# Nine extra contiguous products leave the TensorE stream, and eleven of its large products get another column order

## The chip, the cores and the metric

The kernel runs on one core of one Trainium2 chip. The metric is the device time of one execution in microseconds (us). Each time given for a kernel is the median of several executions; one more execution is taken with the hardware profiler and has a time of its own.

## The reference

One decoder layer (depth 1, model width 2048) is applied to 256 prompt rows and to 8 x 8 = 64 sample rows that share all weights, so 320 rows in all:

```python
xn = rms_norm(x, g_mix)
b_gate, c_gate, h_conv, q, k, v, gate_c, gate_a = split(xn @ w_in)
y_conv = (b_gate * dwconv3(c_gate * h_conv)) @ w_conv_out
y_attn = window_attention(q, k, v, rel_bias, sinks) @ w_attn_out      # window 128, 16 heads, 4 kv heads
h = x + (sigmoid(gate_c) * y_conv + sigmoid(gate_a) * y_attn) @ w_o
hn = rms_norm(h, g_ffn)
h = h + (silu(hn @ w_gate) * (hn @ w_up)) @ w_down                    # inner width 5632
y = rms_norm(h, g_final)
```

The prompt attends in two blocks of 128 queries; the sample rows attend to a cached window of 128 keys and their own 8. Beside y the kernel returns the updated key, value and convolution windows. All data is float32.

## The kernel before, in words

Every large product has the weights as the stationary operand (128 x 128) and all 320 rows as the moving one: 320 columns a matmul. To keep float32 accuracy both sides are split into a rounded part and a remainder, and three products are summed in PSUM: `whi` by `xh_t`, `whi` by `xl_t`, `wlo` by `xh_t`. The weights stream from HBM in 512 KB pieces on SP's queue into `wraw`; ScalarE (ACT) makes `whi`, VectorE (DVE) makes `wlo` (`split_to`, L128 to L130).

TensorE's (PE's) program runs in the order in which it is written. `kv_product` forms keys and values (tiles of 1, 1, 1, 1, 2, 2, ... chunks of 128 features; `k0` is the first chunk of a tile), then come the four products for `q`, then `C`, `H`, `B` in turn four times, then eight rounds of `gc`, `ga`, `yc`, `ya` (gates and the two output projections), `wo`, and two halves of the feed-forward network (`fg`, `fu`, then `dn` for the down projection). All but `kv` and `dn` go through `product` (its matmul is L186; that of `kv` is L372).

Attention is side work: a generator that `tick` advances by one step behind each loaded weight tile. `prompt_attention` has eight units (two heads of one kv head each): `prompt_scores` puts six matmuls of 256 columns (`ps`) into the stream, `prompt_pv` twice 24 small ones (`po`), `sample_attention` 64 scores (`pss`) and 72 value products (`spo`).

Two details matter here. First, the 320 rows lie as five segments of 64, 64 columns of one chunk following those of the last, so that one chunk's moving operand is five runs of 64 elements with a fixed step (`fives`, `rows_in`). Second, `turns` sets the order in which a large product visits its columns: four from the first segment, four from the second, ... and, after all five, the next four of each. PSUM is written in the same order. Matmuls in the program's rows read 128x16x5x4 in that order and 128x320 where the columns are written straight through.

`nudge` (L205 to L207) is a matmul that computes nothing which is used: a contiguous run of 320 elements of `xh_t` by a contiguous 128 of `xl_t` (or `hh_t`, `hl_t`), into a tile of the four-deep `aux` PSUM pool that nobody reads. It stands in nine places: at `k0` of 6 in `kv_product`, before the third `q` product, twice behind `prompt_pv`, behind the last unit's scores, behind the sample's scores, behind the sample's values, and ahead of the first `fu` product of either half.

Of the kernel before, what the change touches and what calls it, by code (L numbers as in the profile page):

```python
# [17 lines left out]
T = TP + NB * TS  # L18
# [8 lines left out]
P = 128  # L27
# [25 lines left out]
def hybrid_layer(ctx: ExitStack, tc: tile.TileContext, a: dict, o: list):  # L53
    nc = tc.nc
# [17 lines left out]
    def ps_aux(name):  # L72
        return aux[0].tile([P, 512], F32, tag="aux", name=name)
# [3 lines left out]
    def u(s):  # L77
        uid[0] += 1
        return f"{s}_{uid[0]}"
# [21 lines left out]
    def turns(ap):  # L101

        return ap.rearrange("p s (i b) -> p i s b", b=4)

    def fives(ap):

        return ap.rearrange("p (s j) -> p s j", s=NS)
# [24 lines left out]
    def load_cols(w, k0, n, c0, behind=()):  # L132
# [4 lines left out]
            split_to(hi[:, :n, :], lo[:, :n, :], raw[:, :n, :])  # L137
        return hi, lo

    mark = {}  # L140
    side_work = [None]
    pending = []
    last = {}
# [28 lines left out]
    def product(load, nk, xh, xl, name, tiles=None, loaded=None):  # L172

        ps = [ps_acc(u(name)) for _ in range(2)]
        k0 = 0
        for n in tiles or [min(KT, nk - k) for k in range(0, nk, KT)]:
            hi, lo = load(k0, n)
            if loaded:
                loaded()
            order = [(k, c) for k in range(n) for c in range(2)]  # L180
            if k0 + n == nk:
                order.sort(key=lambda kc: kc[1])
            for k, c, i in passes(order, k0 + n == nk):
                kc = k0 + k
                w, x = ((hi, xh), (hi, xl), (lo, xh))[i]
                last["mm"] = nc.tensor.matmul(  # L186
                    turns(fives(ps[c][:, :T])), w[:, k, c * P:(c + 1) * P], turns(x(kc)),
                    start=(kc == 0 and i == 0), stop=(kc == nk - 1 and i == 2),
                )
            k0 += n  # L190
            while pending:
                with after(last["lo"], last["mm"]):
                    pending.pop(0)()
            tick()
        return ps

    def two_parts(src, tags=("ta", "tb")):
# [3 lines left out]
        nc.scalar.activation(hi, src, AF.Copy)  # L201
        nc.vector.tensor_sub(lo, src, hi.bitcast(F32))
        return hi, lo

    def nudge(rows, weights, n=T):  # L205
        x, w = (bass.AP(r.tensor, r.offset, [list(r.ap[0]), [1, m]]) for r, m in ((rows(0), n), (weights(0), P)))
        nc.tensor.matmul(ps_aux(u("nudge"))[:, :n], w, x, start=True, stop=True)  # L207

    def over_partitions(out, parts):
        for i, x in enumerate(parts):  # L210
# [48 lines left out]
    xh, xl = row_tiles(xp, ("xh_t", "xl_t"), KC, LEAD_X, ("xh", "xl"))  # L259
# [26 lines left out]
    def x_load(i, eng=nc.sync):  # L286
# [11 lines left out]
        out=ident, in_=ident, compare_op=ALU.not_equal, fill=1.0, base=0, pattern=[[-1, P]],  # L298
# [47 lines left out]
    def kv_product(tiles, x_after):  # L346

        ps = [ps_acc(u("kv")) for _ in range(4)]
        k0 = 0
        x_prep(0)  # L350
        for i, n in enumerate(tiles):
            if k0 == 6:
                nudge(xh, xl)
            hi, lo = load_kv(k0, n)
            if i == 0:
                x_prep(1)
            for b in x_after.get(i, ()):
                x_load(b)
            order = [(k, c) for k in range(n) for c in range(4)]
            if k0 + n == KC:  # L360
                order.sort(key=lambda kc: kc[1])
            seq = passes(order, k0 + n == KC)
            if i == 0:
                seq.sort(key=lambda kcm: kcm[2])
            for k, c, m in seq:
                kc = k0 + k
                if k0 and (k, c, m) == (0, 3 if n > 1 else 1, 0) and k0 + n < KC:
                    for kk in range(tiles[i + 1]):
                        x_prep(k0 + n + kk)
                    tick()  # L370
                w, x = ((hi, xh), (hi, xl), (lo, xh))[m]
                last["mm"] = nc.tensor.matmul(  # L372
                    turns(fives(ps[c][:, :T])), w[:, k, c * P:(c + 1) * P], turns(x(kc)),
                    start=(kc == 0 and m == 0), stop=(kc == KC - 1 and m == 2),
                )
            k0 += n
            if i == 0:
                tick()
        return ps
# [88 lines left out]
    def at_rows(part):  # L468
# [15 lines left out]
        out=sides[:, 0], in_=sides[:, 0], compare_op=ALU.is_ge, fill=0.0, base=-1, pattern=[[-1, WIN]],  # L484
# [158 lines left out]
    def prompt_attention():  # L643
        units = [(j * 2 + par, gp) for j in range(2) for gp in range(2) for par in range(2)]
        bias, sc, sm, turned, pts = {}, {}, {}, {}, {}
        bias[0] = bias_load(*units[0])
        for i in range(len(units) + 3):
            if i < len(units):
                if i + 1 < len(units):
                    bias[i + 1] = bias_load(*units[i + 1])  # L650
                sc[i] = prompt_scores(*units[i], bias.pop(i))
                if i + 1 == len(units):
                    nudge(xh, xl)
                yield
                sm[i] = prompt_softmax(*units[i], sc[i])
            if 0 <= i - 3 < len(units):
                pts[i - 3] = prompt_sides(i - 3, turned.pop(i - 3))
            yield
            if i >= 4 and i % 4 == 2:
                for n in (i - 5, i - 3):  # L660
                    kv, gp = units[n]
                    prompt_pv(kv // 2, gp, (pts.pop(n - 1), pts.pop(n)))
                nudge(xh, xl)
            if 0 <= i - 1 < len(units):
                turned[i - 1] = prompt_norm(i - 1, sc.pop(i - 1), *sm.pop(i - 1))
            yield
# [3 lines left out]
    def sample_attention(sm):  # L670
# [3 lines left out]
        s = sm.tile([P, NB, W2], F32, name="s_s")  # L674
# [6 lines left out]
        for base in range(0, NB, 3):  # L681
            ps = ps_aux(u("pss"))
            n = min(3, NB - base)
            for b in range(base, base + n):
                o0 = (b - base) * W2
                for kv in range(NKV):
                    j, par = kv // 2, kv % 2
                    rows = slice(par * 64, par * 64 + 64)
                    nc.tensor.matmul(
                        ps[kv * 32:(kv + 1) * 32, o0:o0 + W2], qs[rows, j, b, :], kf[rows, b, j, :],  # L690
                        start=True, stop=True,
# [2 lines left out]
                s[:, base:base + n, :], ps[:, 0:n * W2].rearrange("p (b k) -> p b k", b=n),  # L694
                flip(bias_s).unsqueeze(1).to_broadcast([P, n, W2]),
            )
        nudge(xh, xl)
        yield
        yield

# [49 lines left out]
        for j in range(2):  # L750
            for par in range(2):
# [4 lines left out]
                    start=True, stop=False,  # L756
                )
        for b in range(NB):
            cv = cvs.pop(b)
            for j in range(2):  # L760
                for par in range(2):
# [3 lines left out]
                        cv[:, kv * HD:(kv + 1) * HD], ptw[:, kv, b * 32:(b + 1) * 32],  # L765
                        start=False, stop=(b == NB - 1),
                    )
        nudge(xh, xl)
        yield
        for j in range(2):  # L770
            src = pos[j][:, 0:256].rearrange("p (b g t) -> p g b t", b=NB, g=GRP)
            o = LEAD_A + j * 4 * at_row
            rows = at_t[:, o:o + 4 * at_row].rearrange("p (g w) -> p g w", g=GRP)[:, :, -2 * JS:]
# [42 lines left out]
    for j in range(2):  # L816
        for gp in range(2):
            if (j, gp) == (1, 0):
                nudge(xh, xl)
            ps = in_pair(O_Q + (j * 2 + gp) * CW, "q")  # L820
            pending.append(lambda j=j, gp=gp, ps=ps: q_out(j, gp, ps))
    side_work[0] = attention()
# [2 lines left out]
    for cp in range(4):  # L825
        c_sb = []
        ps = in_pair(O_C + cp * CW, "C")
# [4 lines left out]
        ps = in_pair(O_H + cp * CW, "H")  # L832
        conv = []
        for c in range(2):
# [13 lines left out]
            n = UL - 2  # L848
# [10 lines left out]
        ps = in_pair(O_B + cp * CW, "B")  # L859
# [17 lines left out]
    mm = mp_.enter_context(tc.tile_pool(name="mm", bufs=1, side="right"))  # L877
# [9 lines left out]
    for mp in range(8):  # L887
        c0 = mp * CW
        sg = {}
        for nm, off, tag in (("gc", O_GC, "ta"), ("ga", O_GA, "tb")):  # L890
            ps = in_pair(off + c0, nm)
# [26 lines left out]
    for mp in range(8):  # L918
# [5 lines left out]
        for c in range(2):  # L924
            k = mp * 2 + c
# [101 lines left out]
    for half in range(2):  # L1027
# [4 lines left out]
        for fpair in range(nf // 2):  # L1032
            c0 = (f0 + fpair * 2) * P
            psg = product(
                lambda k0, n: load_cols(w_g, k0, n, c0), KC,
                hh, hl, "fg",
            )
            if half == 0 and fpair == 0:
                pss = ps_aux("pss2")
                over_partitions(pss[:, :T], two_parts(hacc, ("tc", "td")))  # L1040
                rstd_of(pss[:, :T], [P, T], "r2", hp, out=rb2)
            gs = []
            for c in range(2):
                t, t2 = tmp("ta", "gs")[:, :T], tmp("tb", "sg")[:, :T]
                nc.vector.tensor_mul(t, psg[c][:, :T], rb2)
                last["sig"] = nc.scalar.activation(t2, t, AF.Sigmoid)
                nc.vector.tensor_mul(t, t, t2)
                nc.vector.tensor_mul(t, t, rb2)
                gs.append(t)
            if fpair == 0:  # L1050
                nudge(hh, hl)
            psu = product(
                lambda k0, n: load_cols(w_u, k0, n, c0), KC,
                hh, hl, "fu",
            )
            for c in range(2):
                nc.vector.tensor_mul(gs[c], psu[c][:, :T], gs[c])
                f = fpair * 2 + c
                (first, rest), row = parts_of(gs[c]), a_move(f)
                nc.scalar.activation(row[:, :, JR:JT], rest, AF.Copy)  # L1060
                last["hi"] = nc.scalar.activation(row[:, :, 0:JR], first, AF.Copy)
                nc.vector.tensor_sub(row[:, :, JT:], rest, row[:, :, JR:JT].bitcast(F32))
                last["lo"] = nc.vector.tensor_sub(placed(a_low(f)), first, row[:, :, 0:JR].bitcast(F32))
                if half == 1:
                    nc.scalar.activation(a_first(f), gs[c][:, 0:P], AF.Copy)
# [109 lines left out]
    for c in range(4):  # L1175
        k = E0 // P + c
# [147 lines left out]
```

## Time and profile before

| | before |
|---|---|
| median of 3 runs | 1593.76 us (1593.33 to 1593.9) |
| the profiled execution's own time | 1593.85 us |
| its span, first to last instruction | 1592.1 us |
| PE busy | 1583.2 us, 99% of the span |
| PE's weight loads busy | 1547.1 us |
| DVE, ACT busy | 890.9 us, 645.9 us |
| granted TensorE clock | 0.998 |

Matmuls overlap: a product of 320 columns shows 301 ns from its start to its end, and the next starts 140 ns after it. So busy time is a union of overlapping pieces, and the pace of the stream is read from starts: from the chain of waits, which merges consecutive work of one line into a row of start, length and count (the rows' starts are ends of the work before them, so they lie some 0.16 us behind the starts of the timeline), and from the timeline.

### The profile page before, as it was taken

The page shows a single profiled execution, that of the slowest core. Times are in us where ns is not written, and L with a number is a line of the kernel's source. Part 1 is how long each engine was busy: PE and PEld are TensorE (multiplying, and loading weights), DVE is VectorE, ACT ScalarE, POOL GpSimd, SP SyncE. Part 2 cuts the span into 40 slices and gives each one's busy share as a digit, 9 for nine tenths or more (in the row PEclk, how much of TensorE's full clock was granted, in tenths as well). Part 3 has the DMA queues.
Part 4 walks back from the last instruction along what each step waited for, and adds up shares of the span by engine and source line. Part 5 has one row for each costly group of instructions (what it writes and reads, how often), then busy time and mean ns, then how long its engine had stood idle before and what let it go on. Part 6 is the DMA issues. An engine that isn't in the chain of part 4 may idle for free.

```text
span 1592.1 us, 26453 instructions
## 1 busy us (share of the span) xinstructions
PE 1583.2 (99%) x10899; PEld 1547.1 (97%) x10899; DVE 890.9 (56%) x1314; ACT 645.9 (41%) x917; POOL 133.2 (8%) x213
## 2 busy tenths in 40 slices
PE   9999999999999999999999999999999999999998
PEld 9999999999999999999999999998888999999887
DVE  7879765445555445556555555553444455555556
ACT  7554443333333333344333333333333334444443
POOL 1414332000000003320000000000000000000021
PEclk9999999999999999999999999999999999999999
DMA  7757566544455544455554545555555454445663
GB/s 271 207 182 218 171 211 203 166 154 155 157 159 159 159 156 155 155 158 159 157 154 155 159 158 159 159 156 161 155 155 157 157 159 158 156 155 157 190 180 131
DMA packets 77648, 266.06 MB, mean 167 GB/s; under 512 B 9832, under 2 KB 13112, under 8 KB 77400
## 3 DMA queue, kind: packets, MB, share of 16 engines
q1 hardware_dynamic: 71736, 249.99, 50.2%
q0 software_dynamic: 5360, 13.84, 3.0%
q8 instruction: 85, 1.39, 0.4%
q10 hardware_dynamic: 432, 0.56, 0.1%
q14 instruction: 35, 0.29, 0.1%
HBM read 257.27 MB, written 9.04 MB: 167 GB/s over the span
## 4 chain that ended last, share of the span: by engine, by line
PE 99%; DMA 0%; DVE 0%; ACT 0%; issue 0%; SPq 0%; DVEq 0%
PE fu L186 19%; PE fg L186 19%; PE dn L997 9%; PE wo L186 7%; PE gc L186 7%; PE ga L186 7%; PE dn L1005 6%; PE C L186 3%; PE B L186 3%; PE H L186 3%; PE q L186 3%; PE ya L186 3%; PE yc L186 3%; PE dl L1001 2%; PE kv L372 2%; PE dn L1162 1%
## 5 line engine op out<-in xcount | busy, mean ns | idle before, releaser
L130 DVE TENSOR_TENSOR wlo<-wraw,whi 128x1024 fp32r<-128x1024 f32 (+1 forms) x460 | 563.1, 1225 | 564.5 <-ACT whi L129 453.4
L129 ACT ACTIVATE whi<-wraw 128x1024 fp32r<-128x1024 f32 (+1 forms) x460 | 485.5, 1056 | 722.0 <-PE fu L186 129.5
L186 PE MATMUL fu<-hh_t,whi 128*128 128x320 f32 x704 | 205.0, 301 | 0.0
L186 PE MATMUL fu<-hl_t,whi 128*128 128x320 f32 x704 | 205.0, 301 | 0.0
L186 PE MATMUL fg<-hh_t,whi 128*128 128x320 f32 x704 | 205.0, 301 | 0.0
L186 PE MATMUL fg<-hl_t,whi 128*128 128x320 f32 x704 | 205.0, 301 | 0.0
L186 PE MATMUL fu<-hh_t,wlo 128*128 128x320 f32 x704 | 158.8, 301 | 0.0
L186 PE MATMUL fg<-hh_t,wlo 128*128 128x320 f32 x704 | 158.8, 301 | 0.0
L997 PE MATMUL dn<-a_t,whi 128*128 128x512 f32 x640 | 155.2, 382 | 0.0
L186 PEld LDWEIGHTS fu<-hh_t,whi 128*128 128x128 f32 x704 | 131.7, 187 | 0.0
L186 PEld LDWEIGHTS fu<-hl_t,whi 128*128 128x128 f32 x704 | 131.7, 187 | 0.0
L186 PEld LDWEIGHTS fg<-hh_t,whi 128*128 128x128 f32 x704 | 131.7, 187 | 0.0
L186 PEld LDWEIGHTS fg<-hl_t,whi 128*128 128x128 f32 x704 | 131.7, 187 | 0.0
L997 PEld LDWEIGHTS dn<-a_t,whi 128*128 128x128 f32 x640 | 115.4, 187 | 16.5 <-issue 1.2
L186 PEld LDWEIGHTS fg<-hh_t,wlo 128*128 128x128 f32 x704 | 116.1, 187 | 0.0
L186 PEld LDWEIGHTS fu<-hh_t,wlo 128*128 128x128 f32 x704 | 116.1, 187 | 0.0
L1005 PEld LDWEIGHTS dn<-a_t,wlo 128*128 128x128 f32 x640 | 97.7, 188 | 6.9
L1005 PE MATMUL dn<-a_t,wlo 128*128 128x320 f32 x640 | 103.4, 301 | 0.0
L186 PE MATMUL gc<-xh_t,whi 128*128 128x320 f32 x256 | 74.5, 301 | 0.0
L186 PE MATMUL gc<-xl_t,whi 128*128 128x320 f32 x256 | 74.5, 301 | 0.0
L186 PE MATMUL ga<-xh_t,whi 128*128 128x320 f32 x256 | 74.5, 301 | 0.0
L186 PE MATMUL ga<-xl_t,whi 128*128 128x320 f32 x256 | 74.5, 301 | 0.0
(317 smaller groups left out, 2695.7 us busy)
## 6 DMA issues: line engine op xcount, KB each, us to landing
wraw<-in_w_in_dram SPq DMA_DIRECT2D x128, 512.0 KB, 3.9
wraw<-in_w_gate_dram SPq DMA_DIRECT2D x88, 512.0 KB, 3.8
wraw<-in_w_up_dram SPq DMA_DIRECT2D x88, 512.0 KB, 3.7
wraw<-in_w_down_dram SPq DMA_DIRECT2D x88, 512.0 KB, 3.7
wraw<-in_w_o_dram SPq DMA_DIRECT2D x32, 512.0 KB, 3.8
wraw<-in_w_conv_out_dram SPq DMA_DIRECT2D x16, 512.0 KB, 3.6
wraw<-in_w_attn_out_dram SPq DMA_DIRECT2D x16, 512.0 KB, 3.7
wraw<-in_w_kv_dram SPq DMA_DIRECT2D x6, 512.0 KB, 7.5
```

The costliest lines, as they stand in the source:

```text
L129: last["hi"] = nc.scalar.activation(hi, src, AF.Copy)
L130: last["lo"] = nc.vector.tensor_sub(lo, src, hi.bitcast(F32))
L186: last["mm"] = nc.tensor.matmul(turns(fives(ps[c][:, :T])), w[:, k, c * P:(c + 1) * P], turns(x(kc)), start=(kc == 0 and i == 0), stop=(kc ...
L372: last["mm"] = nc.tensor.matmul(turns(fives(ps[c][:, :T])), w[:, k, c * P:(c + 1) * P], turns(x(kc)), start=(kc == 0 and m == 0), stop=(kc ...
L997: nc.tensor.matmul(turns(placed(ps[c])), parts[k][0][:, cs], turns(a_move(k)), start=k == 0, stop=False)
L1001: nc.tensor.matmul(low, a_low(k), parts[k][0], start=k == 0, stop=k == nf - 1 and c0 < E0)
L1005: last["mm"] = nc.tensor.matmul(turns(placed(ps[c])[:, :, 0:JT]), parts[k][1][:, cs], turns(a_move(k)[:, :, 0:JT]), start=False, stop=k == ...
L1162: nc.tensor.matmul(turns(placed(ps[c])[:, :, JR:]), held[k][0][:, cs], turns(a_move(k)[:, :, JR:]), start=k == 0, stop=k == nf - 1,)
```

## The change

`nudge` and its nine calls go. A wrapper `weigh` issues the large products, and `once(way)` makes the next product that it issues, and only that one, use another column order: "plain" (five segments one after the other, 128x320) or "long" (32 columns from each segment in turn, then the other 32 of each, 128x2x5x32). It computes the same sums into the same places of PSUM. The plain order is asked for in nine places: at `k0` of 1, 4 and 6 in `kv_product`, before the third `q` product, twice behind `prompt_pv`, behind the sample's scores, and for the first `fu` product of either half. The long order is asked for in two: behind the scores of the first unit (where no nudge stood) and behind the sample's values. Behind the scores of the last unit nothing stands in the nudge's place.

```diff
+    walks = {"plain": lambda ap: ap, "long": lambda ap: ap.rearrange("p s (i b) -> p i s b", b=32)}
+    walk = [None]
+
+    def weigh(out, w, x, **kw):
+        way = walks.get(walk[0], turns)
+        walk[0] = None
+        last["mm"] = nc.tensor.matmul(way(fives(out)), w, way(x), **kw)
+
+    def once(way):
+        walk[0] = way
...
-                last["mm"] = nc.tensor.matmul(
-                    turns(fives(ps[c][:, :T])), w[:, k, c * P:(c + 1) * P], turns(x(kc)),
+                weigh(
+                    ps[c][:, :T], w[:, k, c * P:(c + 1) * P], x(kc),
...
-    def nudge(rows, weights, n=T):
-        x, w = (bass.AP(r.tensor, r.offset, [list(r.ap[0]), [1, m]]) for r, m in ((rows(0), n), (weights(0), P)))
-        nc.tensor.matmul(ps_aux(u("nudge"))[:, :n], w, x, start=True, stop=True)
...
-            if k0 == 6:
-                nudge(xh, xl)
+            if k0 in (1, 4, 6):
+                once("plain")
...
-                if i + 1 == len(units):
-                    nudge(xh, xl)
+                if i == 0:
+                    once("long")
...
                     prompt_pv(kv // 2, gp, (pts.pop(n - 1), pts.pop(n)))
-                nudge(xh, xl)
+                once("plain")
...
-        nudge(xh, xl)
+        once("plain")
         yield
         yield
 
...
-        nudge(xh, xl)
+        once("long")
         yield
         for j in range(2):
...
             if (j, gp) == (1, 0):
-                nudge(xh, xl)
+                once("plain")
...
             if fpair == 0:
-                nudge(hh, hl)
+                once("plain")
```

PE's program loses nine matmuls (9683 rows become 9674), and no instruction of the other engines is added or removed; on DVE one addition of four elements a partition moves past its neighbour. Three places on PE show what moved; the names are the program's, with its running numbers.

PE, the first unit's scores, before:

```order
L186 MATMUL C_1130<-xh_t,wlo_1134 128x16x5x4
L562 MATMUL ps_135_1180<-k_498,at_t 128x256 x2
L565 MATMUL ps_136_1181<-k_498,at_t 128x256
L562 MATMUL ps_135_1180<-k_498,at_t 128x256 x2
L565 MATMUL ps_136_1181<-k_498,at_t 128x256
L186 MATMUL C_1129<-xh_t,whi_1195 128x16x5x4
L186 MATMUL C_1129<-xl_t,whi_1195 128x16x5x4
```

and in the change:

```order
L146 MATMUL C_1126<-xh_t,wlo_1130 128x16x5x4
L569 MATMUL ps_133_1176<-k_496,at_t 128x256 x2
L572 MATMUL ps_134_1177<-k_496,at_t 128x256
L569 MATMUL ps_133_1176<-k_496,at_t 128x256 x2
L572 MATMUL ps_134_1177<-k_496,at_t 128x256
L146 MATMUL C_1125<-xh_t,whi_1191 128x2x5x32
L146 MATMUL C_1125<-xl_t,whi_1191 128x16x5x4
```

The count of matmuls is the same; the first `C` product behind the scores goes in pieces of 32 columns.

PE, the last unit's scores, before:

```order
L186 MATMUL B_2097<-xh_t,wlo_2170 128x16x5x4
L562 MATMUL ps_297_2198<-k_498,at_t 128x256 x2
L565 MATMUL ps_298_2199<-k_498,at_t 128x256
L562 MATMUL ps_297_2198<-k_498,at_t 128x256 x2
L565 MATMUL ps_298_2199<-k_498,at_t 128x256
L207 MATMUL nudge_2211<-xh_t,xl_t 128x320
L186 MATMUL B_2096<-xh_t,whi_2215 128x16x5x4
```

and in the change:

```order
L146 MATMUL B_2093<-xh_t,wlo_2164 128x16x5x4
L569 MATMUL ps_294_2192<-k_496,at_t 128x256 x2
L572 MATMUL ps_295_2193<-k_496,at_t 128x256
L569 MATMUL ps_294_2192<-k_496,at_t 128x256 x2
L572 MATMUL ps_295_2193<-k_496,at_t 128x256
L146 MATMUL B_2092<-xh_t,whi_2207 128x16x5x4
```

The nudge is gone and every large product behind these scores is in the usual order.

PE, the end of the sample's values, before:

```order
L763 MATMUL spo_3180<-ptw,cv_2819 64x32 x2
L763 MATMUL spo_3181<-ptw,cv_2819 64x32 x2
L207 MATMUL nudge_3218<-xh_t,xl_t 128x320
L186 MATMUL B_3148<-xh_t,whi_3222 128x16x5x4
L186 MATMUL B_3148<-xl_t,whi_3222 128x16x5x4
```

and in the change:

```order
L770 MATMUL spo_3168<-ptw,cv_2807 64x32 x2
L770 MATMUL spo_3169<-ptw,cv_2807 64x32 x2
L146 MATMUL B_3136<-xh_t,whi_3208 128x2x5x32
L146 MATMUL B_3136<-xl_t,whi_3208 128x16x5x4
L146 MATMUL B_3137<-xh_t,whi_3208 128x16x5x4
```

The nudge is gone, and the first `B` product, which was to follow it, takes its place in pieces of 32 columns. In the other places the pattern is the same with a plain product: the first large product behind the old nudge reads 128x320.

More of the change, by code (lines that the diff above doesn't have):

```diff
@@ L371, in kv_product @@
                 w, x = ((hi, xh), (hi, xl), (lo, xh))[m]
-                last["mm"] = nc.tensor.matmul(
-                    turns(fives(ps[c][:, :T])), w[:, k, c * P:(c + 1) * P], turns(x(kc)),
+                weigh(
+                    ps[c][:, :T], w[:, k, c * P:(c + 1) * P], x(kc),
                     start=(kc == 0 and m == 0), stop=(kc == KC - 1 and m == 2),
```

## The prediction

> **What bounds the kernel now.** The page first: who is busy, and what ended last.
>
> ```profile
> span 1592.1 us, 26453 instructions
> PE 1583.2 (99%) x10899; PEld 1547.1 (97%) x10899; DVE 890.9 (56%) x1314; ACT 645.9 (41%) x917; POOL 133.2 (8%) x213
> PE 99%; DMA 0%; DVE 0%; ACT 0%; issue 0%; SPq 0%; DVEq 0%
> L129 ACT ACTIVATE whi<-wraw 128x1024 fp32r<-128x1024 f32 (+1 forms) x460 | 485.5, 1056 | 722.0 <-PE fu L186 129.5
> ```
>
> PE is busy for all of the span and is 99% of the chain, and ACT, which makes the weights' parts, sits idle for 722.0 us, most of it until PE gives a buffer back. Then the waits of PE over the whole span:
>
> ```profile
> PE wm L305 <- PEq L1304: 0.8, 1, 0.8
> PE kv L372 <- ACT whi L129: 0.6, 1, 0.6
> ```
>
> After the start PE waits once, for 0.6 us. So the time is the number of matmuls times their pace, and a change of PE's program tells at full price. The pace is read from the chain in order of time (start, length, line, count), which has the work around the edited places in rows of whole stretches:
>
> ```profile
> 16.01 0.15 PE nudge L207
> 16.15 16.81 PE kv L372 x120
> ...
> 39.90 0.49 PE prb L211 x2
> 40.39 20.16 PE q L186 x144
> ...
> 60.55 0.15 PE nudge L207
> 60.70 26.90 PE q L186 x192
> ...
> 90.96 0.23 PE ps L562 x2
> 91.20 0.12 PE ps L565
> 91.31 0.23 PE ps L562 x2
> 91.55 0.12 PE ps L565
> 91.66 10.24 PE C L186 x72
> 101.91 0.24 PE ps L562 x2
> ...
> 102.26 0.24 PE ps L562 x2
> ...
> 102.62 10.10 PE H L186 x72
> ...
> 166.12 0.34 PE nudge L207
> ...
> 169.84 0.23 PE ps L562 x2
> 170.08 0.12 PE ps L565
> 170.19 0.23 PE ps L562 x2
> 170.43 0.12 PE ps L565
> 170.54 0.15 PE nudge L207
> 170.69 6.73 PE B L186 x48
> ...
> 190.86 6.72 PE H L186 x48
> 197.58 2.74 PE po L629 x24
> ...
> 256.43 0.34 PE nudge L207
> 256.77 10.10 PE B L186 x72
> 266.88 13.44 PE gc L186 x96
> ```
>
> The rule is 13.44 us for 96 products, 140.0 ns each: the **even pace**. The stretch behind the first unit's scores is another thing: 72 products in 10.24 us, 142.2 ns each, the **slow pace**. It lasts, by that mean, over the whole stretch; the next scores end it (10.10 us for the next 72, 140.3 ns with the settling behind the scores). So the stream has a state that outlives the matmul that set it, and it costs 2.2 ns a product. The only other such stretch is at the start, from the product after the wait of 0.6 us to the first nudge (timeline):
>
> ```profile
> 7.45 0.30 PE L372 MATMUL kv<-xl_t,whi 128*128 128x320 f32 x1
> 15.84 0.31 PE L207 MATMUL nudge<-xh_t,xl_t 128*128 128x320 f32 x1
> ```
>
> 59 products in 8.39 us, 142.2 ns each; behind the nudge 120 in 16.81, 140.1. That row shows what a nudge does: one contiguous matmul ends the slow pace. Of the nine, only this one visibly ends it; the one at 60.55 stands in a stream that was even already.
>
> **The change part by part**, against the profiled execution's own 1593.85 us, which is 0.09 above the median of the runs.
>
> *Nine matmuls fewer.* A nudge has a slot of 0.15 in a running stream (16.01, 60.55, 170.54 and two more) and 0.34 behind small matmuls (166.12, 256.43 and two more). The 0.34 doesn't go: it holds the restart of full-size work, which the next large product will then pay. What goes is nine slots at the even pace, 9 x 0.140 = -1.26; at the last unit's scores nothing replaces the nudge, so its settling goes too, 0.02: **-1.28**. Bounds: -1.26, and -1.33 with five slots at the 0.15 of the rows.
>
> *Three places with a new odd product* (`k0` of 1 and 4, first scores). A nudge in an even stream takes 0.15, 0.01 more than a slot, and the 192 products behind the one at 60.55 take 26.90 us, 0.02 over 192 x 0.140. The plain or long product pays the same in its own slot: 3 x 0.03 = **+0.09**, between 0 and 0.13 (the settling of 0.04 that the rows' rounding allows). The other eight pay it today. A plain product is no nudge, though: it reads five runs of 64 where the nudge read 320 in one. Nearest to it are two contiguous products that the program needs anyway, ahead of the nudge at 710.69:
>
> ```profile
> 710.39 0.29 PE pss L211 x2
> 710.69 0.15 PE nudge L207
> 710.84 13.45 PE fu L186 x96
> ```
>
> 0.15 each, as a nudge. The Trainium skill ("Advanced Engine Details and Errata", PSUM Cachelines) says that any non-contiguous access pattern in PSUM slows matmuls significantly. By that the plain products would be cheaper than the usual ones, which write runs of four, and this part would be a gain; here 140 ns in runs of four stands against 0.15 us contiguous, so the trace does not agree, and the size is some 0.1 us either way.
>
> *The slow stretch at the start.* With a plain product at 7.20 the 59 products run evenly: 59 x 2.2 ns = **-0.13**; 0 if it has no effect. PE may not run into its data instead: the third chunk's `whi` is made by
>
> ```profile
> 7.87 0.62 ACT L129 ACTIVATE whi<-wraw 128x512 fp32r<-128x512 f32 x1
> ```
>
> at 8.49, and its first product starts at 7.45 + 11 x 0.142 = 9.01, with 0.5 us to spare.
>
> *First scores.* If the long product restores the even pace, the 72 products behind it gain 10.24 - 10.10 = 0.14. But what went into these scores was the even stream that a nudge had left, and the slow pace came out; the scores of the second unit met the slow pace and left the even one. The same even stream would now reach the second unit's scores and lose 0.14 there. **0**; bounds -0.14 (both even) and +0.02 (neither changes).
>
> *Last scores.* Here the removal is not free. The stream that enters them is even and comes from a nudge (166.12), as it was before the first scores, and the six scores look alike: 0.23, 0.12, 0.23, 0.12 both times, 0.70 in sum, while the pairs (x2) of the second unit's take 0.24. Behind the first came the slow pace. Behind the last stands a nudge, and with it gone the slow pace would last until `po` at 197.58: 4 x 48 = 192 products (170.69 to 197.58) at 2.2 ns, **+0.42**. Bounds 0 and 0.42; I take the upper, since the first unit's rows are the nearest.
>
> *The other eight places.* A plain (or, behind the sample's values, a long) product takes the nudge's slot and must leave the even pace as the nudge did: **0**. The stakes behind three of them are long: products from 256.77 to the `pss` at 710.39 (453.6 us / 0.140 = 3240), then
>
> ```profile
> 710.67:1073.57 362.89, 362.89 (x2592) 1.00 0.50 157
> 1274.52:1467.80 193.28, 193.28 (x1382) 1.00 0.50 158
> ```
>
> 2592 and 1382 products to the `dn` stages (rows of the stages' windows, L186 alone). At 2.2 ns each that is 7.1, 5.7 and 3.0 us; the upper bound of this part is their sum with the shorter places, some 17 us. All nine nudges, `pss` and `prb` (144 products in 20.16 us) were followed by the even pace, hence 0.
>
> *DVE and ACT.* One tiny DVE addition changes place; DVE is idle for 44% of the span. If that cover were gone, its own length would be the price. The nudges' PSUM tiles go too, so scores take tiles that were freed earlier or later by one in a pool of four; no wait of PE on that pool is in the list above, and the pool only gets emptier: 0.
>
> Sum: -1.28 + 0.09 - 0.13 + 0 + 0.42 + 0 = -0.90, so 1592.95 for the profiled execution and 1592.9 for the median.
>
> **The rivals.**
>
> *A. The last scores keep the even pace.* If a plain product leaves another even state than a nudge did, the last scores need not upset it. For it: the stretches behind the second unit to the last but one are even without any nudge. Against it: the equal score rows above. It takes off 0.42, and with the first scores even as well 0.56: 1592.3 to 1592.4. The Trainium skill ("TensorE: Matmul & The Clock Gate", Step-by-step) gives TensorE two independent read ports, so that a weight load takes nothing from a running matmul; by that alone the order would be free everywhere and the sum -1.26, in the same place. The slow stretch is against such a reading.
>
> *B. The long product behind the sample's values does not restore the even pace.* This is the case on the other side, slower than before. No run of pieces of 32 is in the trace. The slow pace did arise out of a restart once (7.20), and it lasted across new weight tiles, so gates and projections would keep it until `pss`: 3240 products, +7.1, so 1600.0. It decides from the point where the slow pace lasts for 0.90/0.0022 = 410 products, four rounds of 96. The same with a plain product at `fu` gives 1598.6 (first half) or 1595.9 (second half); both are less likely, since the first stands right behind two contiguous `pss` and the second in a stream that is even already.
>
> *C. The plain product is no reset at all*, so that the change does not do what the nudges did. Then all places between the start and 256 fall to chance, about 1.3 us if all are slow, and the three long ones come on top: up to some 1610. Against it: `prb` and `pss` read other tiles, with other weights, and were followed by the even pace as well.
>
> **How the numbers follow.** The forecast 0.49, A 0.35, B with its sisters 0.12, C 0.04. Times within 0.2% (3.2 us, about what a measurement of this kernel can tell from no change) hold the forecast and A. All parts at their best make -1.33 - 0.13 - 0.14 = -1.60, so faster by 3.2 us is out of reach for anything named here: 0.01. Slower: B but for the milder sister, and C, 0.14. The range runs from 1591.7 (all at its best, less 0.5 for the spread of the runs shown) to 1594.4 (the forecast with one short place slow, 192 products or 0.4, and one more such place and the spread), which leaves out B and C. Forecast and A by themselves span 1592.2 to 1593.4.
>
> **What would show it.** No nudge rows, 10,890 matmuls, and the chain's large rows still 13.44 for 96. The kv row from 7.20 on at 140 ns. Behind the last scores 6.83, 13.65 and 6.83 for 48, 96 and 48 say slow, 6.72, 13.44, 6.72 say rival A. Behind the sample's values `gc` at 13.65 for 96 says B. The forecast is wrong if any 96 products take 13.6 or more in the chain after 260 us, or if the sum of gains in the rows up to 260 us isn't near 0.6 us.

## The result: slower by 0.36%, out of one place

The changed kernel takes 1599.31 us (median of 6, 1598.83 to 1599.59), the kernel before 1593.72 (6 runs, 1593.33 to 1593.95): a ratio of 1.0036, 95% interval 1.0026 to 1.0046. The forecast was 1592.9 with a range to 1594.4. The profiled execution took 1599.47 us. Its page has the same shape as before, with one product stream of 99% and nine matmuls fewer:

```profile
span 1597.8 us, 26435 instructions
PE 1589.0 (99%) x10890; PEld 1553.1 (97%) x10890; DVE 890.6 (56%) x1314; ACT 646.4 (40%) x917; POOL 132.1 (8%) x213
```

The chain of waits in order of time (start, length, line, count) says where the time went. Of the changed kernel, around the two places of the long product, the last scores and the first `fu`:

```profile
91.33 10.10 PE C L146 x72
...
102.14 8.00 PE H L146 x57
...
169.93 6.74 PE B L146 x48
176.66 13.44 PE C L146 x96
190.10 6.72 PE H L146 x48
...
252.36 1.01 PE spo L760 x8
...
255.36 10.44 PE B L146 x72
265.80 13.65 PE gc L146 x96
279.45 13.65 PE ga L146 x96
...
702.70 13.65 PE fg L146 x96
716.36 0.31 PE pss L218 x2
716.67 13.46 PE fu L146 x96
```

Up to the sample's values (`spo`, 252.36 against 253.43) the change had gained 1.07 us. From the product behind them on, 96 products take 13.65 us and no longer 13.44: the slow pace of 142.2 ns, which holds through `gc`, `ga`, `yc`, `ya`, `wo` and the first `fg`. It ends at `pss` and the plain product behind it, 716.36 against 710.39: 5.97 us lost where 1.07 had been won, so 7.04 us in this one stretch. That is 3240 products by 2.2 ns (7.1) less the slot of 0.14 of the nudge. Behind it `fu` is even again, as it is to the end.

The rows ahead of it differ from the forecast too. Behind the first scores 72 products take 10.10 us, not 10.24, and the 57 of `H` behind the second unit's take 8.00, 140.4 ns each; behind the last scores 6.74, 13.44 and 6.72. All of this is even, as rival A had it.

### The profile page after: what moved, and what is told of

Same layout as the page of the kernel before. It is cut to its first block, busy times and chain, and to the rows that moved or that the text cites. A ratio compares the mean times of both kernels' runs of the same rounds, so it can differ in the third digit from the quotient of the medians.

```text
span 1597.8 us, 26435 instructions
## 1 busy us (share of the span) xinstructions
PE 1589.0 (99%) x10890; PEld 1553.1 (97%) x10890; DVE 890.6 (56%) x1314; ACT 646.4 (40%) x917; POOL 132.1 (8%) x213
## 4 chain that ended last, share of the span: by engine, by line
PE 99%; DMA 1%; DVE 0%; ACT 0%; issue 0%; SPq 0%; DVEq 0%; ACTq 0%
PE fg L146 19%; PE fu L146 19%; PE dn L1004 9%; PE ga L146 7%; PE wo L146 7%; PE gc L146 7%; PE dn L1012 6%; PE ya L146 3%; PE yc L146 3%; PE B L146 3%; PE H L146 3%; PE C L146 3%; PE q L146 3%; PE dl L1008 2%; PE kv L146 1%; PE dn L1169 1%
## 5 line engine op out<-in xcount | busy, mean ns | idle before, releaser
L146 PE MATMUL wo<-m_l,whi 128*128 128x320 f32 x256 | 75.6, 304 | 0.0
```

What stands on the lines that cost most here:

```text
L146: last["mm"] = nc.tensor.matmul(way(fives(out)), w, way(x), **kw)
```

## Experiments

The medians of the kernel before, run beside these, were 1593.36 to 1593.41 us.

### One product in another order

```diff
-        once("long")          # behind the sample's values
+        once("plain")
```

> The changed kernel with the plain order, not the long one, for the first product behind the sample's values. Theory 1 (the long product at this place is what leaves the slow pace; a plain one leaves an even pace here as it does behind the two prompt_pv and the sample's scores): gc, ga and wo at 13.44 us for 96 products, 3240 x 2.2 ns = 7.1 us less than the change, so 1592.1 to 1592.3 us. Theory 2 (the stream reaches this place in another state than before, and the restart behind the 72 small matmuls goes slow whatever order follows): 13.65 for 96, 1599.3 us.

Nine runs took 1591.78 to 1592.32 us and one 1599.06; median 1591.96, ratio to before 0.9995 (0.9985 to 1.0004). The chain of the profiled execution behind the values:

```profile
255.12 10.32 PE B L146 x72
265.44 13.44 PE gc L146 x96
```

Theory 1. The order of one product in 10,890 makes 7.3 us (1591.96 against 1599.24 in the next experiment, which ran beside it). The odd run is longer by 7.1 us, as long as the slow stretch of the change, so a plain product here probably repairs nearly always and not always; where that run lost its time was not seen, since it has no profile. The ratio's interval holds 1 because that run counts in it.

### No odd product at all

```diff
-        once("long")          # behind the sample's values
```

> The changed kernel with no odd product behind the sample's values: the usual order goes on at once. Theory 1a (a restart is slow unless an odd product repairs it, and the long one merely failed to repair it): slow, 13.65 us for 96 products, 1599.2 us. Theory 1b (the long product itself brings the slow pace about): even, 13.44 for 96, 1592.1 us.

1599.24 us (1598.75 to 1599.45); 1.0035 (1.002 to 1.005). Behind the values:

```profile
255.33 10.43 PE B L146 x72
265.77 13.65 PE gc L146 x96
```

Theory 1a: here the restart (the first large products behind small matmuls) is slow without help, and the long product failed to help. It did not bring the slow pace about.

### The nudge kept in this place alone

```diff
-        once("long")
+        nudge(xh, xl)
```

> The changed kernel with the separate contiguous matmul kept behind the sample's values alone. Theory 1 (only the kind of the first product behind the restart decides): even behind it, 13.44 us for 96, one slot of 0.14 us more than with a plain product there, 1592.3 us. Theory 2 (what happened upstream decides): slow, 1599.5 us.

1592.17 us (1591.62 to 1593.0); 0.9992 (0.9982 to 1.0003); `gc` at 13.44 for 96. With a nudge the restart is even behind the same work upstream, in all eight runs.

### The last scores without a nudge, in the kernel before

```diff
-                if i + 1 == len(units):
-                    nudge(xh, xl)
```

> The kernel before with the nudge behind the last unit's scores taken out and nothing else changed; it tells the term of +0.42 us from rival A. Theory 1 (the prediction's: the even stream that a nudge leaves is upset by six scores): the 48, 96 and 48 products behind these scores take 6.83, 13.65 and 6.83 us, 1593.85 - 0.16 + 0.42 = 1594.1 us. Theory 2 (these scores upset nothing): 6.73, 13.44 and 6.72 us, 1593.7 us.

1593.73 us (1593.51 to 1594.09); 1.0002 (0.9992 to 1.0012). The times can't tell these theories apart; the chain can:

```profile
165.86 0.34 PE nudge L207
166.21 3.37 PE B L186 x24
...
170.28 6.82 PE B L186 x48
177.11 13.65 PE C L186 x96
190.76 6.83 PE H L186 x48
197.59 2.74 PE po L629 x24
```

Theory 1, within 0.01 us. In the stream that the nudge at 165.86 leaves, six scores do set the slow pace. In the changed kernel the same scores met another even stream, and didn't (6.74, 13.44, 6.72). So there are two even states. They can be seen: means of one matmul by group, in the window 217 to 250 us, of the kernel before and then of the changed one.

```profile
L186 PE MATMUL C<-xh_t,whi 128*128 128x320 f32 x32 | 9.3, 301 | 0.0
```

```profile
L146 PE MATMUL C<-xh_t,whi 128*128 128x320 f32 x32 | 9.3, 302 | 0.0
```

301 ns from start to end in the one, 302 in the other, both started every 140.0 ns; in the slow pace the mean is 303 or 304, by group:

```profile
L146 PE MATMUL gc<-xh_t,whi 128*128 128x320 f32 x245 | 72.1, 303 | 0.0
```

(the changed kernel, window 270 to 690). The state can thus be read in any window of a trace that holds no restart; below, the three are called the 301 state, the 302 state and the slow one.

The 302 state is not something that a plain product makes. In the changed kernel `q` runs at 301 behind its plain product (window 65 to 86), and 302 begins behind the first scores, where the long product stands. The kernel before has 302 as well (window 157 to 162), from the second unit's scores to the nudge behind the first `prompt_pv`, which turns it into 301. In this order:

```profile
L146 PE MATMUL q<-xh_t,whi 128*128 128x320 f32 x51 | 14.9, 301 | 0.0
```

```profile
L186 PE MATMUL B<-xh_t,whi 128*128 128x320 f32 x7 | 2.0, 302 | 0.0
```

The plain products behind both `prompt_pv` and the sample's scores leave the 302 standing: the changed kernel has it in every window that was read between 103 us and the sample's values. That is what went missing with the nudges. But a plain product can bring 301 too: `val_plain` has it behind the values (window 270 to 690).

```profile
L146 PE MATMUL ga<-xh_t,whi 128*128 128x320 f32 x256 | 74.5, 301 | 0.0
```

Nor does a nudge always bring 301: in the run of this section, without the last scores' nudge, the one behind the second `prompt_pv` met the slow pace and left 302 (window 202 to 212).

### Other orders at the other restarts

```diff
-        once("long")          # behind the sample's values
+        nudge(xh, xl)
...
-                once("plain")     # behind both prompt_pv
...
-        once("plain")         # behind the sample's scores
```

> The changed kernel with the nudge kept behind the sample's values (even there, 1592.2 us), and now the usual order, no odd product, behind both prompt_pv and behind the sample's scores. Theory 1 (every restart behind small matmuls goes slow unless a contiguous product repairs it): 24, 96 and 264 products behind them at 142.2 ns, the row of 96 behind the sample's scores at 13.65 us, 0.05 + 0.2 + 0.6 = 0.85 us more, 1593.0 us. Theory 2 (these three restarts are even of themselves, only the one behind the sample's values is slow): 13.44 us for 96, 1592.2 us.

1593.25 us (1592.83 to 1593.47); 0.9998 (0.9988 to 1.0009).

```profile
165.08 3.57 PE B L146 x24
...
169.36 6.83 PE B L146 x48
176.18 13.65 PE C L146 x96
...
199.41 6.94 PE H L146 x48
...
215.06 7.03 PE B L146 x48
222.08 13.65 PE C L146 x96
```

Neither theory. Behind the first `prompt_pv` the stream restarted evenly (3.57 for 24 holds the 0.2 of every restart), and the scores then set the slow pace, as they do in the 301 state; behind the second it came back even; behind the sample's scores it came back slow.

```diff
-        once("long")          # behind the sample's values
+        nudge(xh, xl)
...
-                once("plain")     # behind both prompt_pv
+                once("long")
...
-        once("plain")         # behind the sample's scores
+        once("long")
```

> The same with the long order in those three places. Theory 1 (a long product repairs no restart): slow as with the usual order, 1593.0 us. Theory 2 (it is the place, not the order): even, 13.44 us for 96 behind the sample's scores, 1592.2 us.

1592.65 us (1591.99 to 1592.8); 0.9994 (0.9984 to 1.0005). In the profiled execution, which was the fastest:

```profile
164.88 3.62 PE B L146 x24
...
198.85 7.03 PE H L146 x48
205.88 6.83 PE B L146 x48
...
214.70 6.93 PE B L146 x48
221.63 13.44 PE C L146 x96
```

Slow behind both `prompt_pv` (3.62, 7.03 and 6.83), even behind the sample's scores. So neither the usual nor the long order has the same result at every restart, while the plain order had the even one at all three of these places in every profile that had it there. For the long order the state that comes in makes the difference. Ahead of both `prompt_pv` it was 302 (windows 157 to 162 and 171 to 195):

```profile
L146 PE MATMUL B<-xh_t,whi 128*128 128x320 f32 x8 | 2.4, 302 | 0.0
```

```profile
L146 PE MATMUL C<-xh_t,whi 128*128 128x320 f32 x32 | 9.3, 302 | 0.0
```

Ahead of the sample's scores it was the slow one, and 302 came out (windows 200 to 212 and 217 to 250). The usual order can't be sorted so: out of 302 it restarted evenly behind the first `prompt_pv` and slowly behind the sample's values (`val_usual`).

### The odd products inside the running stream taken out

```diff
-        once("long")          # behind the sample's values
+        nudge(xh, xl)
...
-            if k0 in (1, 4, 6):
-                once("plain")
...
-                if i == 0:
-                    once("long")
...
-            if (j, gp) == (1, 0):
-                once("plain")
...
-            if fpair == 0:
-                once("plain")
```

> The changed kernel with the nudge kept behind the sample's values, and the usual order in the places that lie in a running stream: the three of kv_product, the third q product, the first unit's scores and the first fu products; the plain ones behind the restarts stay. Theory 1 (only kv and the first scores need one): the start slow until prb at 39 us, or from the wait on, some 60 to 230 products, +0.1 to +0.5 us; 72 products behind the first scores at 10.24 us and the second unit's at 10.10; fu, fg and q at 13.44 for 96: 1592.4 to 1592.8 us. Theory 2 (every place needs its odd product): fg and fu at 13.65 as well, +8.7 us, 1601 us.

1597.86 us (1597.68 to 1599.18); 1.003 (1.0018 to 1.0042).

```profile
5.90 10.11 PE kv L146 x72
...
39.67 47.04 PE q L146 x336
...
90.77 10.24 PE C L146 x72
...
101.72 10.09 PE H L146 x72
...
708.90 0.30 PE pss L222 x2
709.20 13.66 PE fu L146 x96
722.86 13.65 PE fg L146 x96
...
1278.68 13.44 PE fu L146 x96
```

Theory 1 for the first scores (10.24, then 10.09), for `q` (140.0 ns each) and for the second half, where the feed-forward network ran evenly. Wrong for the first half: behind the two contiguous `pss`, without the plain product, 2592 products run slowly, 5.7 us, which is what this kernel loses to the one with a nudge at the values (1592.17). `kv` happened to start evenly here (72 products in 10.11), so its plain products can't be valued from this run. Two of the six runs took longer, 1598.61 and 1599.18 us; the profile is of another one, so why is open.

### Two odd products in a row behind the values

In these three kernels `once` takes a list, one order for each of the next products.

```diff
-        once("long")          # behind the sample's values
+        once("plain", "plain")
```

> The changed kernel with two plain products in a row behind the sample's values. With one, nine of ten runs took 1591.8 to 1592.3 us and one 1599.06. Theory 1 (one plain product repairs this restart only just, and a second makes it sure): all runs at 1592.0 us, 0.02 us over one plain product. Theory 2 (the rare run is lost before these products, or by anything else): one run in some ten is at 1599 us here too.

1591.95 us (1591.46 to 1592.55), ten runs, none near 1599; 0.999 (0.998 to 0.9999).

```diff
-        once("long")          # behind the sample's values
+        once("usual", "plain")
```

> The changed kernel with a product in the usual order and then a plain one behind the sample's values. Seen so far: a plain product right behind a wait of the start left the slow pace twice, and the next plain one, in the running slow stream, ended it both times. Theory 1 (a plain product in a running slow stream always ends it; only as the first product of a restart it may fail): all runs even, 1592.0 us, none at 1599. Theory 2 (the repair needs the place right behind the restart): slow, 1599.2 us.

1592.04 us (1591.6 to 1592.41), ten runs, none near 1599; 0.9992 (0.9982 to 1.0001). One of the two plain products of the start that this expectation speaks of, in the kernel with the usual order at the restarts (timeline):

```profile
11.72 0.41 PE L146 MATMUL kv<-xh_t,whi 128*128 128x320 f32 x1
11.97 0.30 PE L146 MATMUL kv<-xl_t,whi 128*128 128x320 f32 x1
...
15.24 0.31 PE L146 MATMUL kv<-xh_t,whi 128*128 128x320 f32 x1
```

The one at 11.72 came behind a gap (it started 0.24 us after the product before it, not 0.14); the 23 products from 11.97 to the next plain one at 15.24 take 3.27 us, 142.2 ns each.

```diff
-        once("long")          # behind the sample's values
+        once("long", "long")
```

> The changed kernel with two long products in a row behind the sample's values. Theory 1 (a long product in a running slow stream ends it, as the one behind the first scores seems to do; it failed here because it was the first of a restart): even, 13.44 us for 96, 1592.0 us. Theory 2 (pieces of 32 end no slow stream): 13.65 for 96, 1599.3 us.

1591.86 us (1591.36 to 1592.51), eight runs; 0.999 (0.998 to 1.0); `gc` at 13.44. All three agree with theory 1: as the second product behind the restart, a plain and a long one both left an even stream. What the first of each pair left can't be read from one product. The long order isn't wrong as such; here it was put on the first product of a restart. With one run in ten lost behind one plain product, twenty without a loss behind a second chance don't yet prove the second sure.

### What the restart brings with it

Why was the restart behind the values bad for the long order? First the long product alone, in the kernel before:

```diff
-        nudge(xh, xl)         # behind the sample's values
+        once("long")          # with weigh and once as in the change
```

> The kernel before with one edit: a long product in place of the nudge behind the sample's values, all other nudges kept, so that the stream comes here in the even state that nudges leave. Theory 1 (the restart with a long product is slow whatever stream came before): gc at 13.65 us for 96, 1593.4 - 0.1 + 7.1 = 1600.4 us. Theory 2 (it was the even state left by the plain products upstream that made it slow): 13.44, 1593.3 us.

1593.26 us (1592.76 to 1593.66); 0.9997 (0.9987 to 1.0008), eight runs, all even; behind the values:

```profile
256.37 10.29 PE B L146 x72
266.65 13.44 PE gc L146 x96
```

Theory 2: the same product in the same place, and no loss. So something upstream decides. The last experiment makes one edit upstream, in the changed kernel:

```diff
-        once("plain")         # behind the sample's scores, 40 us ahead
+        nudge(xh, xl)
```

> The changed kernel with one edit 40 us ahead of the place that went slow: the separate contiguous matmul back behind the sample's scores, in place of the plain product; the long product behind the sample's values stays. Theory 1 (two even states: plain products leave one with 302 ns a matmul, nudges one with 301, the small matmuls carry it on, and a long product restarts evenly out of the second alone): products of 301 ns before the sample's values, gc at 13.44 us for 96 behind them, 1599.3 - 7.2 + 0.14 = 1592.2 us. Theory 2 (only the order of the first product at the restart counts, or the state further up): slow as in the change, 1599.5 us.

1592.13 us (1591.6 to 1592.61), ten runs; 0.9992 (0.9982 to 1.0001). The group of `H` in the window 240 to 250 us, ahead of the values, and the chain behind them:

```profile
L146 PE MATMUL H<-xh_t,whi 128*128 128x320 f32 x21 | 6.1, 301 | 0.0
```

```profile
255.57 10.29 PE B L146 x72
265.86 13.44 PE gc L146 x96
```

Theory 1. One matmul more, 264 products and 72 small ones ahead of the long product, turns 1599.3 into 1592.1; the ten times lie all below the change's six. The changed kernel had 302 in that window:

```profile
L146 PE MATMUL H<-xh_t,whi 128*128 128x320 f32 x20 | 5.8, 302 | 0.0
```

Sorted by the state ahead, the long order (the pair of long products aside) has one result at each restart that a profile shows: slow out of 302 (three times: behind the values in the change and behind both `prompt_pv` in `restarts_long`), 301 out of 301 (twice: the two kernels of this section) and 302 out of the slow pace (once). What is not taken apart is the state from the rest that the nudge does: it also takes a tile of the `aux` PSUM pool and puts what follows 0.14 us later.

## Why the prediction was wrong, step by step

**The bound and the price of a slow product: right.** PE's program sets the time, a slow product costs 2.2 ns, and 3240 of them 7.1 us (7.04 found). DVE, ACT and the PSUM pool stayed out of it.

**The step that failed: "The other eight places: 0".** Seven of the eight held in the changed kernel. The one behind the sample's values did not, and it had the longest stretch behind it: 96 products took 13.65 us there and not 13.44, 7.04 us in all. The step took the even pace for one state, and asked of an odd product only that it leave this pace. The nudges behind `prompt_pv` and the sample's scores did more: they turned 302 into 301, or kept 301. The plain products in their places left 302 standing, and out of it a long product restarts slowly. The step also rested on rows of nudges and of `pss` and `prb`, none of which is in pieces of 32. And `pss` was no evidence for contiguous products: a nudge stood right behind it, and with no odd product there the slow pace followed (13.66). Rival B named place, price and product, 0.12 with its sisters; with A's 0.42 and the first scores' gain off, its 1600.0 becomes 1599.4, against 1599.31. What it lacked is the reason. It took the outcome for a matter of the long order at a restart; the long order restarts evenly in this place out of the 301 state (18 runs in two kernels) and slowly out of the 302 state (six of the change).

**The last scores, +0.42: right for the kernel before, wrong for the change.** The rows of the first unit were read rightly (6.82, 13.65, 6.83 without the nudge), but the stream in question was at 302, no longer at the 301 of a nudge. Rival A, "another even state", is what happened, and the scores were even; only that the plain product did not make this state but left it standing. The two misses rest on one thing: the prediction granted in A that the stream may be in another even state without the nudges, and didn't carry that over to the restart behind the values, where it cost 7 us.

**The first scores, 0: mis-sized.** The long product there works (10.10), and leaves the 302 state, which the second unit's scores do not upset (8.00 for 57): the -0.14 of the lower bound.

**Nudges out and new odd products: right in sum.** -1.28 and +0.09 were part of the forecast; the kernel with one plain product behind the values has everything else of the change, and its median lies 1.40 us below the kernel before. The prediction's terms with A and both scores even give -1.46. The start's -0.13 is in this sum, but it isn't shown apart: whether `kv` starts slowly differs from one execution to the next.

**The range** left out the only cases in which a long stretch goes slow. They had 0.16 between them for the three places that have more than a thousand products behind them, one of which got an untried order; in hindsight that was too little.

## What to carry to other kernels

When a saturated stream has a state that costs a per cent or two (1.6% here) and lasts, weigh each edit by what runs behind it until the next reset (here 72 products in one place and 3240 in another), not by its own length. An edit that leaves the pace alone may still change the state, and the harm can show at a later place, so read the pace of whole stretches in the trace and try each place for itself in several executions. Where one reset may fail, a second one in the running stream costs about 0.01 us (a contiguous product's 0.15 against 0.14): with two plain products behind the sample's values the change is 0.10% faster than the kernel before (0.01 to 0.2%), 1591.95 us.

## What the runs showed of the hardware

A stream of equal 320-column matmuls on TensorE ran in three states, all at a granted clock of 0.998 or 0.999: two at 140.0 ns from start to start (301 and 302 ns from start to end) and one at 142.2 (303 or 304 by group). Once entered, a state held for thousands of matmuls, through other weights, other inputs and other PSUM tiles. Six scores turned the 301 state into the slow one (10.24, 13.65), the slow one into the 302 state (10.09 behind 10.24), and left the 302 state as it was. Work of 2 to 3 us in small matmuls didn't wipe out the difference between the two even states: behind it a long product went on at 301 out of the one and slowly out of the other. What in the hardware keeps the state is open: the runs show which edits change it, not what it is. Why the usual order restarts evenly behind `prompt_pv` and slowly behind the sample's scores and values was not settled either, nor why one run in ten behind a single plain product was slow.
